# Making the weights' low halves on VectorE alone in a two-layer hybrid decoder on one core

## The chip, the cores and the metric

The kernel runs on one core of one Trainium2 chip. What is measured is the device time of one execution in microseconds. Five engines are spoken of: TensorE (PE, with PEld for its weight loads), VectorE (DVE), ScalarE (ACT), GpSimd (POOL) and SyncE (SP), which issues most of the DMAs.

## What is computed

The reference runs two layers of a decoder on 256 positions of width 1024, in float32. Cut to its spine:

```python
def reference(x, mem, ...):
    for layer in range(2):
        h = rmsnorm(x, norm_mix[layer])
        if layer == 0:   # RG-LRU and sparse attention side by side
            mix = even_mixer(h, ...)
        else:            # Mamba-2: conv of x/B/C, chunked scan, gate, grouped norm
            mix = mamba2(h, od_w_in[0], od_conv_w[0], ...)
        x = x + mix
        x = x + cross_attn(rmsnorm(x, norm_cross[layer]), rmsnorm(mem, norm_mem[layer]), ...)
        h = rmsnorm(x, norm_ffn[layer])
        x = x + (swiglu(h, ff_w13[0], ff_w2[0]) if layer == 0   # FF 2816
                 else moe(h, moe_router[0], moe_w13[0], moe_w2[0]))  # top 2 of 8, FF 3584
    return x
```

## The kernel before

**Weights.** All large weights are cut on the host into units of 128 x 2048 float32 (1 MB). The class `Stream` brings them in the order in which they are used: `_dma` issues the loads on SP into buffers named `raw`; `pieces` (line 214) turns a unit into a high half `wh` and a low half `wl`; `limit` sets how many units may stand split ahead of their use (up to three). `advance` splits as many as there is room for, `one` a single unit, and `get` hands a unit to its product and calls `advance`. A high half is the weight rounded to the matmul's format by ScalarE (line 223), and a low half is what the rounding lost, `raw - wh`, one subtraction with both inputs and the output in SBUF (line 226). "A low" below is one such subtraction for one half unit, 128 x 1024 elements. Every product is then three matmuls (`mm3`, lines 433 to 435): high by high, and the two cross terms of high and low. So TensorE needs both halves of a unit before it gets past the unit's first matmuls. Units with a gain (the cross-attention's key and value weights) take their low from line 235, on VectorE, and the units `gates`, `ck` and `cv` aren't split at all.

**Who makes a low half** is said by a table of cuts, three numbers for each piece: first column, last column, and 0 for VectorE or 1 for GpSimd. Line 238 chooses the table:

- `CUTS_D`, the default: first half VectorE, second half GpSimd.
- `CUTS_P`: both halves GpSimd. For `POOL_UNITS`, the first four units `xs` of the Mamba mixer's x part, and for the `one` in the second layer's cross-attention (line 1417).
- `CUTS_M` and `CUTS_E`: both halves VectorE. For unit 3 of the first mixer's output, for the units split inside `pair` (line 580), and for all units of the experts (`m13`, `m2`).
- `CUTS_0`, four quarters on GpSimd, for the very first unit (line 1180); and two units at the experts' entry have both halves on GpSimd by tables of their own (in `ahead` of the router and in the experts' opening).

**Order.** Nothing reorders the program: each engine's instructions run in the order in which the Python emits them. A step of the kernel (a product, an attention stage) calls `get`, whose `advance` emits the lows of the unit three ahead at that point, so a low stands in its engine's queue between instructions of the stage that happens to run then.

**The stages that the change touches**, in their order: the first mixer, the first cross-attention, the dense SwiGLU, the Mamba mixer and the second cross-attention. After that the experts run for more than half of the span, with all their lows on VectorE already.

**The Mamba mixer.** First come the products for the step sizes dt and for B and C (`bc`), then per group of channels x (`xs`) and the gate z. A convolution follows each `bc` and `xs` product (`conv`, lines 844 to 850): ScalarE scales the accumulator in PSUM, then VectorE adds three shifted copies of it (line 848: one input in PSUM, one in SBUF), and `run_between` puts one step of the softplus of dt (line 812, all in SBUF) after each. One step later `conv_silu` (line 1608) has ScalarE's tanh and VectorE's product of it with the convolution (line 1609, all in SBUF). The accumulators in PSUM are four, so TensorE can run ahead of this chain by that much. The softplus ends in `m_a`, which TensorE needs for the cumulative sums (line 1575). While a `bc` unit is multiplied, an `xs` unit is split.

Of each group then `mb_xt` (line 1657 on) makes `m_xd` and `m_xs` (lines 1667, 1670, on VectorE) and `m_y` (line 1669, on GpSimd) from the transposed x, TensorE takes `m_xd` at line 1697 and `m_xs` at line 1709.

**Cross-attention.** `soft` takes row maxima from PSUM on VectorE (`x_mx`, line 1375), `post` divides, `av_t` transposes; the query product `xq` is put between these steps, and the next units are split meanwhile. A norm's `xn` (line 474) and the split of its transposed result (`hl`, line 430) come before the products that follow.

Of the kernel before, what the change touches and what calls it, by code (L numbers as in the profile page):

```python
# [29 lines left out]
NRAW, NRAW1, NRAW2, NRAW3 = 4, 2, 5, 2  # L30
TRACE = None
CUTS_0 = ((0, 512, 1), (512, 1024, 1), (1024, 1536, 1), (1536, 2048, 1))
CUTS_D = ((0, 1024, 0), (1024, 2048, 1))
CUTS_P = ((0, 1024, 1), (1024, 2048, 1))
POOL_UNITS = [("xs", u) for u in range(4)]
CUTS_M = ((0, 1024, 0), (1024, 2048, 0))
CUTS_E = ((0, 1024, 0), (1024, 2048, 0))

PCOLS = dict(mix0=8, mix1=8, cross0=8, cross1=8, mem0=8, mem1=8, ffn0=8, ffn1=8,
             rgw=32, rgb=8, ba=8, bx=8, lam=8, qn=1, kn=3, xqn=2, xkn=2, pos=32,  # L40
# [138 lines left out]
class Stream:  # L179
# [34 lines left out]
    def pieces(self, cuts=None):  # L214
        i = self.ns
        r = self.raw.pop(i)
        h = self.hip.tile([128, 2048], F32R, name="wh")
        l = self.lop.tile([128, 2048], F32R, name="wl")
        self.split[i] = (h, l)
        nc, gains = self.nc, self.gains(self.order[i])  # L220

        def high(a, b):
            nc.scalar.activation(h[:, a:b], r[:, a:b], AF.Copy)  # L223

        def low(a, b, eng):
            (nc.gpsimd if eng else nc.vector).tensor_tensor(l[:, a:b], r[:, a:b], h[:, a:b].bitcast(F32),  # L226
                                                            op=OP.subtract)

        def high_gain(k, g):
            s = slice(k * 512, (k + 1) * 512)  # L230
            nc.scalar.activation(h[:, s], r[:, s], AF.Copy, scale=g)

        def low_gain(k, g):
            s = slice(k * 512, (k + 1) * 512)
            nc.vector.scalar_tensor_tensor(l[:, s], r[:, s], g, h[:, s].bitcast(F32), op0=OP.mult, op1=OP.subtract)
        if gains:
            return [(partial(high_gain, k, g), partial(low_gain, k, g)) for k, g in enumerate(gains)]
        cuts = cuts or (CUTS_M if self.order[i] == ("wo0", 3) else CUTS_E if self.order[i][0] in ("m13", "m2") else CUTS_P if self.order[i] in POOL_UNITS else CUTS_D)
        return [(partial(high, a, b), partial(low, a, b, eng)) for a, b, eng in cuts]

    def limit(self, n):
# [48 lines left out]
def _program(ctx, nc, tc, d, upto):  # L290
# [74 lines left out]
    def add(fn, *units, heavy=False):  # L365
        steps.append((units, fn, heavy or bool(units)))
# [16 lines left out]
    ST = {}  # L383
# [17 lines left out]
    def U(*key, keep=False, lazy=False):  # L401
        return ST["S"].get(tuple(key), keep, lazy)

    def release():
        ST["S"].held -= 1
# [4 lines left out]
    def taken(f):  # L410
        n = len(steps)
        f()
        new = steps[n:]
        del steps[n:]
        return new
# [16 lines left out]
    def mm3(ps, wh, wl, xh, xl, first, last):  # L432
        mm(ps, wh, xh, start=first, stop=False)  # L433
        mm(ps, wh, xl, start=False, stop=False)  # L434
        mm(ps, wl, xh, start=False, stop=last)  # L435
# [7 lines left out]
    def acc():  # L443
        return accp.tile([128, 512], F32, name="acc")
# [4 lines left out]
    H = {}  # L449
# [101 lines left out]
    def pair(ka, kb, emit_a, emit_b, evac, mid=None, wide=True, ahead=None, lazy=False):  # L551
        st = {}
        both = (0, 1) if wide else (0,)

        def s1():
            st["a"] = U(*ka, keep=True, lazy=lazy)
            emit_a(st["a"], 0, both)

        def s2():
            st["b"] = U(*kb, keep=True, lazy=lazy)  # L560
            emit_b(st["b"], 0, both)
            for c in both:
                evac(0, c)

        def s3():
            emit_a(st["a"], 1, both)
            release()
            if mid is None or ahead:
                (ahead or ST["S"].advance)()
            if wide:  # L570
                emit_b(st["b"], 1, (0,))
                evac(1, 0)

        def s4():
            S, cut = ST["S"], []
            if mid is not None:
                mid()
                S._dma()
                if S.room():
                    cut = S.pieces(CUTS_M)  # L580
                    for h, _ in cut:
                        h()
                    n = len(cut) // 2
                    hooks.extend([[l for _, l in cut[:n]], [l for _, l in cut[n:]]])
            emit_b(st["b"], 1, both[-1:])
            evac(1, both[-1])
            release()
            if cut:
                assert not hooks
                S.finish()  # L590
        add(s1, ka)
        add(s2, kb)
        add(s3, heavy=True)
        add(s4, heavy=True)

    def ws(key, h, evac, pool=None):
# [53 lines left out]
    def pair512(name, c, h, evac, ahead=None):  # L650
        st = {}

        def emit(kh):
            def f(w, t, cs):
                xh, xl = h()
                wh, wl = w
                if kh == 0:
                    st[t] = acc()
                for k in range(4):
                    kk = kh * 4 + k  # L660
                    s = slice(t * 128, (t + 1) * 128)
                    ws_ = slice(k * 512, (k + 1) * 512)
                    mm3(st[t], xh[:, kk, s], xl[:, kk, s], wh[:, ws_], wl[:, ws_], kk == 0, kk == 7)
            return f
        pair((name, 2 * c), (name, 2 * c + 1), emit(0), emit(1),
             lambda t, c: evac(t, st[t]), wide=False, lazy=True, ahead=ahead)

    def as1024(name, u0, n, h, evac, mid=None, ahead=None):
        st = {}

        def emit(i):
            def f(w, t, cs):
                xh, xl = h()
                wh, wl = w
                if i == 0 and t + cs[0] == 0:
                    st["ps"] = [acc() for _ in range(4)]
                for c in cs:
                    for k in range(2):
                        kk = i * 2 + k
                        s = slice(t * 128, (t + 1) * 128)  # L680
                        ws_ = slice(k * 1024 + c * 512, k * 1024 + (c + 1) * 512)
                        mm3(st["ps"][t * 2 + c], xh[:, kk, s], xl[:, kk, s], wh[:, ws_], wl[:, ws_],
                            i == 0 and k == 0, i == n - 1 and k == 1)
            return f

        def whole(i):
            def f():
                w = U(name, u0 + i)
                emit(i)(w, 0, (0, 1))
                emit(i)(w, 1, (0, 1))  # L690
            add(f, (name, u0 + i))
        for i in range(n - 2):
            whole(i)
        pair((name, u0 + n - 2), (name, u0 + n - 1), emit(n - 2), emit(n - 1),
             lambda t, c: evac(t, c, st["ps"][2 * t + c]), mid, ahead=ahead)
# [631 lines left out]
    def cross(l, after, mid, fill1, fill2, fill3, late, early=(), ahead=None):  # L1327
        X_ = ExitStack()
        c = {}
        key = f"c{l}"  # L1330
# [73 lines left out]
        def av_m(t):  # L1404
# [9 lines left out]
                s = slice(t * 128, (t + 1) * 128)  # L1414
                split_to(c["h"][:, :, s], c["l"][:, :, s], po)
            return f
        xq = taken(lambda: pair512(f"xq{l}", 0, lambda: H[key], ev_xq, lambda: ST["S"].one(CUTS_P if l else None)))
        wo = taken(lambda: as1024(f"xo{l}", 0, 2, lambda: (c["h"], c["l"]), after, mid, ahead))
        add(open_)
        gap(xq[:2])  # L1420
# [4 lines left out]
        def open2():  # L1425
# [23 lines left out]
        add(lambda: X_.close())  # L1449

    cross(0, lambda t, c, ps: add_X(t, c, ps, N["f0"], (0,)), lambda: N["f0"].tr(0), m1[:1], m1[1:2], m1[2:3],
          lambda c: N["f0"].scale(0))
    if upto == "cross0":
# [411 lines left out]
    def rt_late(c):  # L1865
# [15 lines left out]
        ve.tensor_copy(idb, identb)  # L1881

    cross(1, rt_after, None, [], [], [], rt_late, (rt_open,), ahead)
    if upto == "cross1":
        add(lambda: RT.close())
# [400 lines left out]
```

## Time and profile before

| | |
|---|---|
| median of three runs | 1771.21 us (1771.08 to 1772.83) |
| the profiled execution | 1771.26 us |
| its span | 1769.5 us |
| TensorE's mean granted clock, share of full | 0.988 |
| busy TensorE / its weight loads | 1709.3 / 1436.1 us |
| busy VectorE / ScalarE / GpSimd | 1384.9 / 1162.3 / 346.7 us |
| moved over the span | 489.60 MB, 276 GB/s of HBM traffic |

The busy time of an engine is the time in which one of its instructions ran, stalls inside an instruction included. A wait is time in which an engine had its next instruction but not what that instruction needs. The granted clock of a stretch is the share of TensorE's full rate that the chip allowed in it. In rows with "xN" N instructions of one kind stand together.

### The profile page before, as it was taken

The page shows a single profiled execution, that of the slowest core. Times are in us where ns is not written, and L with a number is a line of the kernel's source. Part 1 is how long each engine was busy: PE and PEld are TensorE (multiplying, and loading weights), DVE is VectorE, ACT ScalarE, POOL GpSimd, SP SyncE. Part 2 cuts the span into 40 slices and gives each one's busy share as a digit, 9 for nine tenths or more (in the row PEclk, how much of TensorE's full clock was granted, in tenths as well). Part 3 has the DMA queues.
Part 4 walks back from the last instruction along what each step waited for, and adds up shares of the span by engine and source line. Part 5 has one row for each costly group of instructions (what it writes and reads, how often), then busy time and mean ns, then how long its engine had stood idle before and what let it go on. Part 6 is the DMA issues. An engine that isn't in the chain of part 4 may idle for free.

```text
span 1769.5 us, 23965 instructions
## 1 busy us (share of the span) xinstructions
PE 1709.3 (97%) x9048; PEld 1436.1 (81%) x9048; DVE 1384.9 (78%) x1669; ACT 1162.3 (66%) x1637; POOL 346.7 (20%) x191
## 2 busy tenths in 40 slices
PE   7999999999998999979999999999999999999997
PEld 7797677899988788767888888888888888888885
DVE  6686756533357898668989999999999999999996
ACT  5646545544444666367777877777777777777874
POOL 4333142444434345345000000000000000000000
PEclk9999999999999999899999999999999999999999
DMA  8555244455563243558999999999999999999980
GB/s 310 215 210 189 94 143 143 162 181 193 179 228 124 93 145 141 204 202 302 386 377 389 370 379 394 368 383 392 374 379 376 374 394 372 385 385 367 402 337 26
DMA packets 74812, 489.60 MB, mean 277 GB/s; under 512 B 11200, under 2 KB 11712, under 8 KB 17472
## 3 DMA queue, kind: packets, MB, share of 16 engines
q1 hardware_dynamic: 67968, 474.36, 70.5%
q0 software_dynamic: 3024, 11.01, 1.7%
q10 hardware_dynamic: 3696, 2.62, 0.5%
q8 instruction: 73, 1.20, 0.3%
q14 instruction: 51, 0.42, 0.1%
HBM read 482.19 MB, written 5.77 MB: 276 GB/s over the span
## 4 chain that ended last, share of the span: by engine, by line
PE 81%; DVE 11%; ACT 4%; issue 2%; POOL 1%; DMA 0%; SPq 0%; ACTq 0%; DVEq 0%; POOLq 0%
PE gu L433 11%; PE gu L435 11%; PE gu L434 11%; PE out L433 6%; PE out L435 6%; PE out L434 6%; PE acc L435 5%; PE acc L433 5%; PE acc L434 5%; PE aux L434 2%; PE aux L435 2%; PE aux L433 2%; DVE wl L226 2%; PE misc L2066 1%; DVE m_y L848 1%
## 5 line engine op out<-in xcount | busy, mean ns | idle before, releaser
L226 DVE TENSOR_TENSOR wl<-raw,wh 128x1024 fp32r<-128x1024 f32 x619 | 747.7, 1248 | 139.3 <-ACT wh L223 138.7
L223 ACT ACTIVATE wh<-raw 128x1024 fp32r<-128x1024 f32 (+1 forms) x722 | 723.1, 1053 | 151.6 <-PE out L435 54.5
L226 POOL TENSOR_TENSOR wl<-raw,wh 128x1024 fp32r<-128x1024 f32 (+1 forms) x103 | 258.9, 2518 | 310.7 <-ACT wh L223 292.3
L433 PE MATMUL gu<-wh,mo_x0h 128*128 128x512 f32 x448 | 178.9, 399 | 0.0
L433 PE MATMUL gu<-wh,mo_x1h 128*128 128x512 f32 x448 | 178.1, 397 | 0.0
L433 PE MATMUL out<-wh,m_xsT 128*128 128x512 f32 x448 | 175.2, 391 | 0.7 <-ACT m_xsT L429 0.7
L435 PE MATMUL gu<-wh,mo_x0l 128*128 128x512 f32 x448 | 175.2, 391 | 0.0
L434 PE MATMUL gu<-wl,mo_x0h 128*128 128x512 f32 x448 | 175.2, 391 | 0.0
L435 PE MATMUL gu<-wh,mo_x1l 128*128 128x512 f32 x448 | 174.7, 390 | 0.0
L434 PE MATMUL gu<-wl,mo_x1h 128*128 128x512 f32 x448 | 174.7, 390 | 0.0
L435 PE MATMUL out<-wh,m_xsT 128*128 128x512 f32 x448 | 174.5, 390 | 0.0
L434 PE MATMUL out<-wl,m_xsT 128*128 128x512 f32 x448 | 174.3, 389 | 0.0
L2114 POOL DMA_DIRECT2D do<-hh x7 | 4.0, 568 | 661.5 <-ACT hh L2113 661.5
L433 PE MATMUL acc<-hh,wh 128*128 128x256 f32 x416 | 122.0, 293 | 0.7 <-DVE m_M L812 0.7
L434 PE MATMUL acc<-hl,wh 128*128 128x256 f32 x416 | 119.1, 286 | 0.5 <-DVE hl L430 0.5
L435 PE MATMUL acc<-hh,wl 128*128 128x256 f32 x416 | 118.8, 286 | 0.0
L434 PE MATMUL aux<-hl,wh 128*128 128x256 f32 x352 | 99.9, 284 | 1.3 <-DVE hl L430 1.3
L433 PE MATMUL aux<-hh,wh 128*128 128x256 f32 x352 | 99.9, 284 | 0.3 <-ACT hh L429 0.3
L435 PE MATMUL aux<-hh,wl 128*128 128x256 f32 x352 | 99.7, 283 | 0.0
L435 PEld LDWEIGHTS gu<-wh,mo_x0l 128*128 128x128 f32 x448 | 84.5, 189 | 18.4
L435 PEld LDWEIGHTS gu<-wh,mo_x1l 128*128 128x128 f32 x448 | 84.1, 188 | 18.3
L433 PEld LDWEIGHTS out<-wh,m_xsT 128*128 128x128 f32 x448 | 84.1, 188 | 18.1 <-ACT m_xsT L429 0.9
(455 smaller groups left out, 3390.5 us busy)
## 6 DMA issues: line engine op xcount, KB each, us to landing
raw<-m SPq DMA_DIRECT2D x265, 1024.0 KB, 7.3
raw<-wd SPq DMA_DIRECT2D x110, 1024.0 KB, 4.8
m_yy<-m SPq DMA_DIRECT2D x24, 1024.0 KB, 7.1
kv<-m SPq DMA_DIRECT2D x24, 1024.0 KB, 7.2
hl<-m SPq DMA_DIRECT2D x23, 1024.0 KB, 7.8
do<-hh POOLq DMA_DIRECT2D x7, 512.0 KB, 8.4
X<-x SPq DMA_DIRECT2D x4, 256.0 KB, 4.8
raw<-wd SPq DMA_DIRECT2D x2, 512.0 KB, 7.7
```

What stands on the lines that cost most here:

```text
L223: nc.scalar.activation(h[:, a:b], r[:, a:b], AF.Copy)
L226: (nc.gpsimd if eng else nc.vector).tensor_tensor(l[:, a:b], r[:, a:b], h[:, a:b].bitcast(F32), op=OP.subtract)
L433: mm(ps, wh, xh, start=first, stop=False)
L434: mm(ps, wh, xl, start=False, stop=False)
L435: mm(ps, wl, xh, start=False, stop=last)
L848: ve.scalar_tensor_tensor(dst[:, s:], src[:, :256 - s], wname(j), dst[:, s:], op0=OP.mult, op1=OP.add)
L2066: pe.transpose(ps[:, j * 128:(j + 1) * 128], mo["hd", e, c][:, j * 128:(j + 1) * 128], ident)
L2114: gp.dma_start(mo["do"][e * 128:(e + 1) * 128], o)
```

## The change

One table, `CUTS`, with both halves on VectorE, takes the place of `CUTS_D`, `CUTS_P`, `CUTS_M`, `CUTS_E` and `POOL_UNITS`. `CUTS_0` for the first unit stays, and so do the two units at the experts' entry. The changed file is four lines shorter, so its line 222 is line 226 of before, and so on down.

```diff
--- before.py
+++ after.py
@@ -30,11 +30,7 @@
 NRAW, NRAW1, NRAW2, NRAW3 = 4, 2, 5, 2
 TRACE = None
 CUTS_0 = ((0, 512, 1), (512, 1024, 1), (1024, 1536, 1), (1536, 2048, 1))
-CUTS_D = ((0, 1024, 0), (1024, 2048, 1))
-CUTS_P = ((0, 1024, 1), (1024, 2048, 1))
-POOL_UNITS = [("xs", u) for u in range(4)]
-CUTS_M = ((0, 1024, 0), (1024, 2048, 0))
-CUTS_E = ((0, 1024, 0), (1024, 2048, 0))
+CUTS = ((0, 1024, 0), (1024, 2048, 0))
 
 PCOLS = dict(mix0=8, mix1=8, cross0=8, cross1=8, mem0=8, mem1=8, ffn0=8, ffn1=8,
              rgw=32, rgb=8, ba=8, bx=8, lam=8, qn=1, kn=3, xqn=2, xkn=2, pos=32,
@@ -235,7 +231,7 @@
             nc.vector.scalar_tensor_tensor(l[:, s], r[:, s], g, h[:, s].bitcast(F32), op0=OP.mult, op1=OP.subtract)
         if gains:
             return [(partial(high_gain, k, g), partial(low_gain, k, g)) for k, g in enumerate(gains)]
-        cuts = cuts or (CUTS_M if self.order[i] == ("wo0", 3) else CUTS_E if self.order[i][0] in ("m13", "m2") else CUTS_P if self.order[i] in POOL_UNITS else CUTS_D)
+        cuts = cuts or CUTS
         return [(partial(high, a, b), partial(low, a, b, eng)) for a, b, eng in cuts]
 
     def limit(self, n):
@@ -577,7 +573,7 @@
                 mid()
                 S._dma()
                 if S.room():
-                    cut = S.pieces(CUTS_M)
+                    cut = S.pieces()
                     for h, _ in cut:
                         h()
                     n = len(cut) // 2
@@ -1414,7 +1410,7 @@
                 s = slice(t * 128, (t + 1) * 128)
                 split_to(c["h"][:, :, s], c["l"][:, :, s], po)
             return f
-        xq = taken(lambda: pair512(f"xq{l}", 0, lambda: H[key], ev_xq, lambda: ST["S"].one(CUTS_P if l else None)))
+        xq = taken(lambda: pair512(f"xq{l}", 0, lambda: H[key], ev_xq, lambda: ST["S"].one()))
         wo = taken(lambda: as1024(f"xo{l}", 0, 2, lambda: (c["h"], c["l"]), after, mid, ahead))
         add(open_)
         gap(xq[:2])
```

On GpSimd the lows of 128 x 1024 go from 99 to 4; VectorE gets 95 more. TensorE, ScalarE and SP issue the same instructions in the same order as before. Three places on VectorE:

The first place is the product of the last `bc` units (`m_BC` is B and C after their activation, `m_y` the convolution, `m_M` the scratch of the softplus). Before:

```order
L848 SCALAR_TENSOR_TENSOR m_y_5283<-acc,m_hw,m_y_5283 128x253
L812 SCALAR_TENSOR_TENSOR m_M<-m_M 128x64
L1609 SCALAR_TENSOR_TENSOR m_BC<-m_th,m_y_5247 128x256
L848 SCALAR_TENSOR_TENSOR m_y_5327<-acc,m_hw,m_y_5327 128x255
L812 SCALAR_TENSOR_TENSOR m_M<-m_M 128x64
L848 SCALAR_TENSOR_TENSOR m_y_5327<-acc,m_hw,m_y_5327 128x254
L812 SCALAR_TENSOR_TENSOR m_M<-m_M 128x64
L848 SCALAR_TENSOR_TENSOR m_y_5327<-acc,m_hw,m_y_5327 128x253
L812 TENSOR_SCALAR m_M<-m_M 128x64
L1609 SCALAR_TENSOR_TENSOR m_BC<-m_th,m_y_5283 128x256
```

And now:

```order
L844 SCALAR_TENSOR_TENSOR m_y_5283<-acc,m_hw,m_y_5283 128x253
L808 SCALAR_TENSOR_TENSOR m_M<-m_M 128x64
L1605 SCALAR_TENSOR_TENSOR m_BC<-m_th,m_y_5247 128x256
L222 TENSOR_TENSOR wl<-raw,wh 128x1024 x2
L844 SCALAR_TENSOR_TENSOR m_y_5327<-acc,m_hw,m_y_5327 128x255
L808 SCALAR_TENSOR_TENSOR m_M<-m_M 128x64
L844 SCALAR_TENSOR_TENSOR m_y_5327<-acc,m_hw,m_y_5327 128x254
L808 SCALAR_TENSOR_TENSOR m_M<-m_M 128x64
L844 SCALAR_TENSOR_TENSOR m_y_5327<-acc,m_hw,m_y_5327 128x253
L808 TENSOR_SCALAR m_M<-m_M 128x64
L1605 SCALAR_TENSOR_TENSOR m_BC<-m_th,m_y_5283 128x256
L844 SCALAR_TENSOR_TENSOR m_y_5363<-acc,m_hw,m_y_5363 128x255
```

Two lows of an `xs` unit, GpSimd's before, stand between line 1609 (now 1605) and the next convolution's first addition. It is so after every second block of `bc`.

The second place is the last group's `mb_xt`, with `m_sz` the gate and `m_yy` the normed output. Before:

```order
L1645 TENSOR_TENSOR m_M<-m_M,m_G 128x512 x4
L226 TENSOR_TENSOR wl<-raw,wh 128x1024
L1609 SCALAR_TENSOR_TENSOR m_xsT<-m_th,m_y_6572 128x256
L1743 SCALAR_TENSOR_TENSOR m_yy<-aux,par,m_yy 128x256 x4
L226 TENSOR_TENSOR wl<-raw,wh 128x1024
L1685 SCALAR_TENSOR_TENSOR m_sz<-m_sz,acc 128x512 x2
L1667 TENSOR_TENSOR m_xd<-m_xs,m_dd 128x512
L1670 TENSOR_TENSOR m_xs<-m_xs,md_dt 128x512 x2
L226 TENSOR_TENSOR wl<-raw,wh 128x1024
```

And now:

```order
L1641 TENSOR_TENSOR m_M<-m_M,m_G 128x512 x4
L222 TENSOR_TENSOR wl<-raw,wh 128x1024 x2
L1605 SCALAR_TENSOR_TENSOR m_xsT<-m_th,m_y_6572 128x256
L1739 SCALAR_TENSOR_TENSOR m_yy<-aux,par,m_yy 128x256 x4
L222 TENSOR_TENSOR wl<-raw,wh 128x1024 x2
L1681 SCALAR_TENSOR_TENSOR m_sz<-m_sz,acc 128x512 x2
L1663 TENSOR_TENSOR m_xd<-m_xs,m_dd 128x512
L1666 TENSOR_TENSOR m_xs<-m_xs,md_dt 128x512 x2
L222 TENSOR_TENSOR wl<-raw,wh 128x1024 x2
```

Each single low has become two, one after the other; the second ones were GpSimd's. `m_y` of `mb_xt` (now line 1665) stays on GpSimd.

The third place is the second cross-attention's first `soft`. Before:

```order
L425 TENSOR_SCALAR rs_tmp<-x_ss 128x4
L1375 TENSOR_REDUCE x_mx<-aux 128x2 x2
L1377 SCALAR_TENSOR_TENSOR x_mx<-x_mx,x_rq 128x4
L1344 COPY x_l<-acc 128x512
L1360 COPY m_xsT<-aux 128x4x128
L425 TENSOR_SCALAR rs_tmp<-x_ss 128x4
L1386 RECIPROCAL x_den<-x_den 128x4
```

And now:

```order
L421 TENSOR_SCALAR rs_tmp<-x_ss 128x4
L222 TENSOR_TENSOR wl<-raw,wh 128x1024 x2
L1371 TENSOR_REDUCE x_mx<-aux 128x2 x2
L1373 SCALAR_TENSOR_TENSOR x_mx<-x_mx,x_rq 128x4
L1340 COPY x_l<-acc 128x512
L1356 COPY m_xsT<-aux 128x4x128
L421 TENSOR_SCALAR rs_tmp<-x_ss 128x4
L1382 RECIPROCAL x_den<-x_den 128x4
```

Two lows, GpSimd's before, now stand ahead of the row maxima `x_mx`.

## Rows read from the trace of the kernel before

**Rows 1.** Page of the profile, part 1: busy us, share of the span, instructions.
```profile
PE 1709.3 (97%) x9048; PEld 1436.1 (81%) x9048; DVE 1384.9 (78%) x1669; ACT 1162.3 (66%) x1637; POOL 346.7 (20%) x191
```

**Rows 2.** Waits of TensorE (waiter, releaser: us in total, times, longest).
```profile
PE aux L1575 <- DVE m_a L812: 3.5, 1, 3.5
PE acc L434 <- POOL wl L226: 2.5, 1, 2.5
PE aux L1593 <- DVE m_M L1586: 2.4, 1, 2.4
PE aux L435 <- DVE m_th L430: 2.2, 1, 2.2
PE aux L1697 <- DVE m_xd L1667: 2.1, 1, 2.1
...
PE aux L434 <- DVE hl L430: 1.3, 1, 1.3
...
PE aux L1709 <- DVE m_xs L1670: 1.1, 1, 1.1
...
PE aux L948 <- DVE c_hs L937: 0.7, 1, 0.7
```

**Rows 3.** Stretches: us; busy of PE, PEld, DVE, ACT, POOL; clock, DMA share, GB/s.
```profile
546.00:552.00 6.00, 6.00 (x52) 6.00 (x51) 5.81 (x11) 3.35 (x6) 2.44 (x1) 1.00 0.21 61
550.00:600.00 50.00, 41.58 (x306) 38.90 (x305) 44.39 (x75) 25.58 (x54) 24.47 (x11) 0.93 0.31 107
600.00:650.00 50.00, 48.76 (x303) 41.91 (x302) 46.21 (x63) 28.84 (x57) 21.62 (x10) 1.00 0.45 160
350.00:400.00 50.00, 50.00 (x358) 47.02 (x357) 16.11 (x21) 22.23 (x30) 20.98 (x10) 1.00 0.53 189
```

**Rows 4.** Timeline of GpSimd in the bc products (start us, us).
```profile
552.24 4.78 POOL L226 TENSOR_TENSOR wl<-raw,wh 128x1024 fp32r<-128x1024 f32 x2 [2.74 <-ACT wh L223]
```

**Rows 5.** Timeline of VectorE there, same columns.
```profile
552.52 2.22 DVE L812 SCALAR_TENSOR_TENSOR m_M<-m_M 128x64 f32<-128x64 f32 x1
554.66 2.64 DVE L1609 SCALAR_TENSOR_TENSOR m_BC<-m_th,m_y 128x256 f32<-128x256 f32 x1
557.22 0.47 DVE L848 SCALAR_TENSOR_TENSOR m_y<-acc,m_hw,m_y 128x255 f32<-128x255 f32 x1
...
558.66 0.21 DVE L812 SCALAR_TENSOR_TENSOR m_M<-m_M 128x64 f32<-128x64 f32 x1
...
565.25 0.47 DVE L848 SCALAR_TENSOR_TENSOR m_y<-acc,m_hw,m_y 128x255 f32<-128x255 f32 x1
```

**Rows 6.** Lines 1609, 848, 226 and 1670 on VectorE: ns min/median/max.
```profile
L1609 DVE SCALAR_TENSOR_TENSOR m_BC<-m_th,m_y x8: 409/812/2640, 545.1 to 572.3; 128x256 f32<-128x256 f32 x8
L848 DVE SCALAR_TENSOR_TENSOR m_y<-acc,m_hw,m_y x72: 377/481/484, 538.2 to 689.7; 128x255 f32<-128x255 f32 x24, 128x254 f32<-128x254 f32 x24, 128x253 f32<-128x253 f32 x24
L226 DVE TENSOR_TENSOR wl<-raw,wh x619: 1199/1218/3414, 19.7 to 1753.1; 128x1024 fp32r<-128x1024 f32 x155
L1670 DVE TENSOR_TENSOR m_xs<-m_xs,md_dt x8: 677/1996/2870, 593.3 to 714.3; 128x512 f32<-128x512 f32 x8
```

**Rows 7.** Timeline of VectorE, last group of the Mamba mixer.
```profile
706.29 2.89 DVE L226 TENSOR_TENSOR wl<-raw,wh 128x1024 fp32r<-128x1024 f32 x1
...
710.30 1.33 DVE L1667 TENSOR_TENSOR m_xd<-m_xs,m_dd 128x512 f32<-128x512 f32 x1
711.73 3.24 DVE L1670 TENSOR_TENSOR m_xs<-m_xs,md_dt 128x512 f32<-128x512 f32 x2
```

**Rows 8.** Timeline of VectorE, end of the first cross-attention.
```profile
317.02 3.56 DVE L474 SCALAR_TENSOR_TENSOR xn<-X,n_rs,f_h 128x512 f32<-128x512 f32 x2
320.50 4.55 DVE L226 TENSOR_TENSOR wl<-raw,wh 128x1024 fp32r<-128x1024 f32 x2
```

**Rows 9.** Stretches of half clock, columns as in rows 3.
```profile
326.50:329.90 3.40, 3.40 (x18) 3.40 (x17) 0.88 (x1) 1.13 (x1) 3.11 (x1) 0.50 1.00 424
...
712.20:725.80 13.60, 12.50 (x43) 9.69 (x42) 7.62 (x9) 0.85 (x2) 1.63 (x1) 0.50 0.22 77
```

## The prediction

> **What bounds the kernel now.** I read the page's busy times first, then TensorE's waits, then windows, and the timelines only where a wait pointed. TensorE is busy 97% of the span [rows 1], so a change on other engines can give back only what TensorE waits, and what it loses at a lower clock. The list of waits [rows 2] names VectorE or GpSimd for nearly every wait in the stages that the change touches; the eight that I use add up to 15.8 us. None is for a transfer of weights, so what the change does to the DMAs' start I cost at nothing: buffers come free when a unit is split, TensorE is what is short, and the DMA share in the four stretches shown is 0.21 to 0.53 [rows 3].
>
> The second thing to see is why VectorE is late. Where GpSimd makes two lows of 2.4 us each, from 552.24 to 557.02 [rows 4], VectorE's step of the softplus takes 2.22 us, and line 1609 takes 2.64 [rows 5]. Undisturbed, the same step takes 0.21 [rows 5] and line 1609 0.41 [rows 6]. These work on SBUF alone. Line 848, which takes one input from PSUM, never took more than 0.484 in 72 instructions [rows 6], whatever GpSimd did. So a low on GpSimd isn't free work beside VectorE: each of these two held VectorE up by (2.22 − 0.21 + 2.64 − 0.41) / 2 = 2.1 us. On VectorE a low takes 1.218 (median of 619 [rows 6]).
>
> **The change, part by part.** It removes 95 lows from GpSimd and adds 95 × 1.218 = 115.7 us of work to VectorE, less the stalls that go. ScalarE's highs stay, in the same order. The sum is made against the profiled execution of 1771.26 us (span 1769.5 and 1.8 around it), which lies 0.05 above the median of the runs.
>
> *Dense SwiGLU.* VectorE is busy 16.1 of 50 us there and TensorE all of them [rows 3]. The cover is VectorE's 34 idle us; GpSimd's ten instructions there, as lows of VectorE, would cost 12.2 [rows 3]. I take 0; without that cover each low would cost its 1.2.
>
> *Products of bc and the first xs.* From one unit's first addition to the next unit's, VectorE's chain takes 565.25 − 557.22 = 8.03 us [rows 5]. TensorE's own pace is 6.00 / 52, some 0.12 us a matmul [rows 3], so 48 × 0.12 = 5.76 for a unit. Without the stalls and with two lows of its own VectorE's cycle is 8.03 − 4.2 + 2.44 = 6.27. Two cycles have this form before `m_a` is wanted, so the wait at line 1575 should fall by 2 × (8.03 − 6.27) = 3.5, which is the whole of it. What comes late next is still the same chain, since 6.27 is over 5.76. Bounds: 0, if the lows put back what the stalls took, and the 5.9 of both waits there (lines 1575 and 1593 [rows 2]). I take **−3.5**.
>
> *The products ahead of bc* wait 2.2 for `m_th` [rows 2]. Its subtraction is of the same size and kind as line 1609; I price its stall likewise at 2.64 − 0.41 = 2.2, and a low now ahead of it at 1.2: **−1.0**, between −2.2 and +1.2.
>
> *End of the first cross-attention.* TensorE waits 1.3 for `hl` [rows 2]. Ahead of it two `xn` take 3.56 where two such operations on SBUF take 2 × 0.68 undisturbed (the least of line 1670 [rows 6]), and two lows take 4.55 for 2.44 [rows 8]. These 4.3 go, and two lows of 2.44 come in: 1.9 earlier, of which the wait can use 1.3. The high half of `hl` is ScalarE's and isn't moved, so I take **−1.0**, between −1.3 and +2.4.
>
> *Last group's* `m_xd` *and* `m_xs`. Before them one low took 2.89 and now two take 2.44; `m_xd` took 1.33 and `m_xs` twice 1.62 [rows 7], undisturbed 0.68 each [rows 6]. That makes `m_xd` 0.45 + 0.65 = 1.1 earlier and `m_xs` 1.9 more. The waits are 2.1 and 1.1 [rows 2]: **−2.2** (1.1 of the first, all of the second), between 0 and −3.2. GpSimd keeps `m_y`, which can still hold `m_xd` up; the earlier groups have other products to run and I cost them at nothing, with TensorE at 48.76 of 50 us [rows 3].
>
> *Second cross-attention.* The 2.5 of waiting for a GpSimd low [rows 2] goes. In exchange two lows stand ahead of `x_mx` and one ahead of a copy that a transpose waits for; I let half of the 2.44 and the 1.2 reach TensorE: −2.5 + 1.2 + 1.2, **0**, between −2.5 and +3.7.
>
> *First mixer.* `c_hs` gets one more low ahead of it where TensorE already waits 0.7 [rows 2]: **+1.2**, between 0 and 1.2. Elsewhere in that mixer TensorE has no listed wait for a low, and I take 0.
>
> Together −3.5 − 1.0 − 1.0 − 2.2 + 0 + 1.2 = −6.5.
>
> *The clock.* Five stretches ran at half the full rate, four of about 3.4 us and one of 13.6 (the first and the last of them: [rows 9]). TensorE was busy 3.4 and 12.5 us in these two, and at full clock would have needed half of that: 1.7 and 6.2. All five together are 4 × 1.7 + 6.2 = 13 at most. They came shortly after TensorE had waited: the first after the 1.3 for `hl`, the third after the 3.5 for `m_a`, the last after the 2.1 and 1.1 of the last group. Where I take a wait away, I expect the stretch behind it to go: bounds 0 and −13. I take the first and third whole and half of the last (its wait shrinks but stays): −1.7 − 1.7 − 3.1 = **−6.5**.
>
> The sum is 1771.26 − 6.5 − 6.5 = **1758.3 us**. Its low end is the bc waits gone whole (−2.4 more) and all five stretches gone (−6.5 more): 1749.
>
> **The rivals.**
> (a) *The waits shrink, and the half clock stays*, because TensorE still waits a little in the same places. For it: every place keeps some wait in my sums. Against: three of the stretches follow just the waits that shrink most. 1771.3 − 6.5 = 1764.8 us.
>
> (b) *No change that shows.* The lows of VectorE stand whole ahead of operations that read PSUM, which never stalled, so that such an operation is 1.2 later per low and nothing comes back for it. If that is so at four of TensorE's waits, 4 × 1.2 gives back 4.9 of the 6.5, and with the clock as it was the time is 1769.6; with one or two places more it is up to 1773. For it: line 848, `x_mx` and `c_hs` are of that kind. Against: in the bc products the stalls are in the same chain as the lows.
>
> (c) *Slower: VectorE becomes the bound from 550 to 650 us.* It is busy 44.39 + 46.21 = 90.6 of 100 us [rows 3], the most of all the stretches that I looked at. GpSimd is busy 46.1 there, at 2.39 a low [rows 4] at most 19 lows. If VectorE's own work were really 90.6, 19 × 1.218 = 23.1 more would make 113.7 and the kernel 13.7 slower, 1785. It decides at 13.7 / 19 = 0.72 us: if a low that leaves GpSimd frees less than that of VectorE's time, VectorE is the bound; at half of it, the time is 1771.3 + 6.9 = 1778. For it: GpSimd works only 20% of the span [rows 1] and takes work that VectorE hardly has room for. Against: 2.1 us freed per low in the two cycles that I measured, and the median 2.0 against a least of 0.68 on line 1670 [rows 6].
>
> One rule speaks for (c). The Trainium skill, Perfetto Trace Analysis, section "Optimizing Scalar/DVE Operations", says that where VectorE is saturated it may pay to offload work to ScalarE or even to GpSimd; by that rule the lows should stay where they are, and the time would be that of (c). The trace disagrees as far as rows 5 go, and the same section's next sentence allows for it: the two engines share a read port, so moving work between them might not help.
>
> That the change doesn't do what it says isn't a rival: the instructions show 95 lows moved.
>
> **How the numbers follow.** The forecast has 0.50, (a) 0.20, (b) 0.15, (c) 0.15. A measurement of this kernel can tell 0.2%, 3.5 us, from no change, so faster means under 1767.7: the forecast and (a), 0.70. (b) is the same, 0.15, and (c) slower, 0.15. The range goes from 1749 to 1772: it holds the forecast with the bounds of its clock term, (a) and most of (b), and leaves out (c).
>
> **What would show it.** In the changed profile no low runs on GpSimd between the first unit and the experts' entry; line 1609 (now 1605) has a median near 0.41 and a largest well under 2; a cycle of bc takes 6.3 us; the wait for `m_a` is under 1 us; the wait for a GpSimd low is gone; and of the half-clock stretches at least two of the five are missing. VectorE's busy time should rise by clearly less than 115.7 us. If line 1609 still takes 2.6 with nothing on GpSimd, my reading of the stalls is wrong. If VectorE is 95% busy or more from 550 to 650 us and TensorE less than before, (c) is right. If the waits are shorter and the span fell by less than 8, the clock term was wrong.

## The result, and the profile after

The changed kernel takes **1751.48 us** (median of four, 1751.32 to 1751.91) against 1771.84 for the kernel before beside it (1771.08 to 1772.83). The ratio is **0.9893, 95% interval 0.9881 to 0.9905**: 20.4 us, or 1.1%, faster. In a later comparison the ratio was 0.9895 (0.9880 to 0.9910). The prediction of 1758.3 had the direction and the mechanism; the gain is half as large again as its 13 us.

Busy times of the page after (columns as in [rows 1]):

```profile
PE 1700.9 (97%) x9048; PEld 1427.0 (82%) x9048; DVE 1419.8 (81%) x1764; ACT 1161.9 (66%) x1637; POOL 106.6 (6%) x96
```

GpSimd went from 346.7 us to 106.6, and VectorE from 1384.9 [rows 1] to 1419.8. That is 34.9 us more for 95 × 1.22 = 116 us of added work, so by this difference some 81 us of VectorE's busy time before were stalls: 81 / 95 = 0.85 us for each low moved, taken over the whole kernel. The operations that stalled, in the view of single lines (ns min/median/max):

```profile
L1605 DVE SCALAR_TENSOR_TENSOR m_BC<-m_th,m_y x8: 416/421/425, 542.9 to 565.9; 128x256 f32<-128x256 f32 x8
```
```profile
L1666 DVE TENSOR_TENSOR m_xs<-m_xs,md_dt x8: 677/689/1347, 585.2 to 701.9; 128x512 f32<-128x512 f32 x8
```
```profile
L887 DVE SCALAR_TENSOR_TENSOR rg_nt<-rg_nt,kv x8: 399/408/421, 100.1 to 121.9; 128x256 f32<-128x256 f32 x8
```

Line 1605 (1609 before) never takes more than 0.425 us, where it reached 2.64 [rows 6]. Line 1666 has a median of 0.69 where it had 2.0 [rows 6]; it reaches 1.35 beside `m_y`, the one large operation that GpSimd kept in that stage. Line 887 belongs to the first mixer's recurrence; before, as line 891, its largest was six times as long:

```profile
L891 DVE SCALAR_TENSOR_TENSOR rg_nt<-rg_nt,kv x8: 398/419/2534, 102.0 to 125.8; 128x256 f32<-128x256 f32 x8
```

The same stretch of the bc products on VectorE (timeline: start us, us):

```profile
550.14 2.35 DVE L222 TENSOR_TENSOR wl<-raw,wh 128x1024 fp32r<-128x1024 f32 x2
552.41 0.48 DVE L844 SCALAR_TENSOR_TENSOR m_y<-acc,m_hw,m_y 128x255 f32<-128x255 f32 x1
...
553.99 0.42 DVE L1605 SCALAR_TENSOR_TENSOR m_BC<-m_th,m_y 128x256 f32<-128x256 f32 x1
...
556.23 2.36 DVE L222 TENSOR_TENSOR wl<-raw,wh 128x1024 fp32r<-128x1024 f32 x2
558.50 0.48 DVE L844 SCALAR_TENSOR_TENSOR m_y<-acc,m_hw,m_y 128x255 f32<-128x255 f32 x1
```

From one unit's first addition to the next it is 558.50 − 552.41 = 6.09 us, for 8.03 before [rows 5] and 6.27 in the prediction, with two lows inside. TensorE's waits (us in total, times, longest):

```profile
PE aux L1589 <- DVE m_M L1582: 3.4, 1, 3.4
...
PE aux L477 <- DVE a_PT L1130: 1.9, 1, 1.9
...
PE misc L2062 <- DVE mo_sg L2055: 1.7, 1, 1.7
...
PE aux L431 <- DVE m_th L426: 0.9, 1, 0.9
...
PE aux L1693 <- DVE m_xd L1663: 0.6, 1, 0.6
...
PE aux L430 <- DVE hl L426: 0.3, 1, 0.3
```

Of the eight waits in [rows 2], those for `m_a` (3.5), for GpSimd's low (2.5), for `m_xs` (1.1) and for `c_hs` (0.7) are gone, `m_th` fell from 2.2 to 0.9, `m_xd` from 2.1 to 0.6, `hl` from 1.3 to 0.3; the one at line 1593 (now 1589) rose from 2.4 to 3.4. Longer, too, is the wait for `a_PT` at the end of the first mixer: 1.9 us where the same operation showed 0.9 before. Busy times by stretch, with the three stretches of half clock that are left in which TensorE works (columns as in [rows 3]; the granted clock is 0.50 inside such a stretch, the lower of the two levels that the rows show, and a window that reaches past it has a little more):

```profile
550.00:600.00 50.00, 45.12 (x341) 41.31 (x341) 45.34 (x90) 27.75 (x60) 2.51 (x2) 0.97 0.37 130
600.00:650.00 50.00, 49.99 (x291) 42.54 (x291) 42.12 (x65) 30.84 (x71) 3.69 (x4) 1.00 0.36 127
547.80:641.20 93.40, 88.51 (x607) 79.40 (x606) 83.27 (x152) 54.34 (x111) 5.50 (x5) 0.98 0.41 146
182.40:189.20 6.80, 6.80 (x14) 3.05 (x15) 2.94 (x5) 1.19 (x2) 0.00 (x0) 0.53 0.00 0
568.20:571.60 3.40, 2.75 (x13) 2.79 (x14) 2.73 (x6) 3.20 (x7) 0.00 (x0) 0.55 0.14 53
776.40:783.20 6.80, 4.92 (x49) 4.86 (x50) 5.23 (x17) 4.29 (x8) 2.13 (x1) 0.53 0.68 258
```

VectorE is busy 45.34 + 42.12 = 87.5 of 100 us from 550 to 650 with all the added work in it, for 90.6 before [rows 3], and TensorE does more: 45.12 and 49.99, for 41.58 and 48.76. The row from 547.80 to 641.20 holds the same 607 matmuls as 550 to 650 before. For these VectorE is busy 83.27 us, with the 16 lows that GpSimd made there before (16 × 1.22 = 19.5 us): 90.6 + 19.5 − 83.3 = 26.8 us of stalls are gone, 1.7 for each low.

TensorE runs the same 9048 matmuls in the same order in both kernels. So the start of the same matmul in the two traces, compared, tells where the time came from (in one profile of each). By place (times are those of the trace before; the third column is the prediction's waits and clock together):

| stretch, us | gained, us | predicted, us |
|---|---|---|
| first mixer, 73 to 140 | +1.4 | −1.2 |
| first mixer's end, 174 to 187 | −4.2 | 0 |
| end of the first cross-attention, 319 to 332 | +2.5 | +2.7 |
| ahead of the bc products, 508 to 536 | +2.3 | +1.0 |
| bc and first xs products, 557 to 592 | +5.8 | +5.2 |
| second group, 600 to 610 | +0.7 | 0 |
| last Mamba group, 702 to 734 | +8.9 | +5.3 |
| second cross-attention, 734 to 788 | 0.0 | 0 |
| experts' entry, 808 to 839 | +1.8 | 0 |

### The profile page after: what moved, and what is told of

It reads as the page before. It is cut to its first block, busy times and chain, and to the rows that moved or that the text cites. A ratio compares the mean times of both kernels' runs of the same rounds, so it can differ in the third digit from the quotient of the medians.

```text
span 1749.5 us, 23766 instructions
## 1 busy us (share of the span) xinstructions
PE 1700.9 (97%) x9048; PEld 1427.0 (82%) x9048; DVE 1419.8 (81%) x1764; ACT 1161.9 (66%) x1637; POOL 106.6 (6%) x96
## 4 chain that ended last, share of the span: by engine, by line
PE 84%; DVE 9%; ACT 4%; issue 1%; DMA 1%; POOL 0%; SPq 0%; ACTq 0%; DVEq 0%
PE gu L429 11%; PE gu L431 11%; PE gu L430 11%; PE acc L431 6%; PE acc L429 6%; PE acc L430 6%; PE out L429 6%; PE out L431 6%; PE out L430 6%; DVE wl L222 3%; PE aux L431 3%; PE aux L430 3%; PE aux L429 2%; PE misc L2062 1%; DVE m_y L844 1%
## 5 line engine op out<-in xcount | busy, mean ns | idle before, releaser
L222 DVE TENSOR_TENSOR wl<-raw,wh 128x1024 fp32r<-128x1024 f32 x714 | 842.8, 1227 | 124.7 <-ACT wh L219 123.9
L429 PEld LDWEIGHTS out<-wh,m_xsT 128*128 128x128 f32 x448 | 84.1, 188 | 18.2 <-ACT m_xsT L425 0.9
L431 PEld LDWEIGHTS out<-wh,m_xsT 128*128 128x128 f32 x448 | 84.1, 188 | 18.0 <-DVE m_xsT L426 0.4
L430 PEld LDWEIGHTS out<-wl,m_xsT 128*128 128x128 f32 x448 | 84.1, 188 | 17.4 <-DVE wl L222 0.3
```

## The experiments

The theory that the prediction states, **held up**: a low on GpSimd stops those operations of VectorE that work on SBUF alone for as long as it runs, some 2 us, and VectorE would make the low itself in 1.2. The rivals were a **latency** theory (TensorE gains because each low is ready sooner), and that the half clock or the later stages come as they like. Ratios below are to the kernel before on the same chip.

**The eight lows of the bc products alone.** In the kernel before:

```diff
-POOL_UNITS = [("xs", u) for u in range(4)]
+POOL_UNITS = []
...
-        cuts = cuts or (CUTS_M if self.order[i] == ("wo0", 3) else CUTS_E if self.order[i][0] in ("m13", "m2") else CUTS_P if self.order[i] in POOL_UNITS else CUTS_D)
+        cuts = cuts or (CUTS_M if self.order[i] == ("wo0", 3) or self.order[i] in [("xs", u) for u in range(4)] else CUTS_E if self.order[i][0] in ("m13", "m2") else CUTS_P if self.order[i] in POOL_UNITS else CUTS_D)
```

> The kernel before, with only the eight lows of the units xs 0 to 3 moved to VectorE (they are the ones made while bc is multiplied). Held-up theory: line 1609 goes back to 0.42 us in the bc products, the cycle of a bc unit falls from 8.03 to about 6.3, the wait for m_a goes, and the time falls by 3.5 us of waiting plus 1.7 to 3.4 us of half clock, so 5 to 7 us, to about 1765. Rival, a latency theory (TensorE gains because a low is ready in 1.2 instead of 2.4 us): nothing waits for these lows, so the time stays within 1 us of before.

1766.02 us, ratio 0.9970 (0.9959 to 0.9982): 5.3 us by the ratio. In the profile:

```profile
L1609 DVE SCALAR_TENSOR_TENSOR m_xsT<-m_th,m_y x16: 414/421/2528, 571.9 to 697.4; 128x256 f32<-128x256 f32 x16
L1609 DVE SCALAR_TENSOR_TENSOR m_BC<-m_th,m_y x8: 411/418/424, 545.3 to 569.0; 128x256 f32<-128x256 f32 x8
```

Line 1609 doesn't stall any more for `m_BC`, whose stage has no low on GpSimd now, and still does for `m_xsT`, whose later units have. The wait for `m_a` fell from 3.5 to 0.6 us, and from one unit's first addition to the next it is 6.1 us.

**All but these eight.** In the changed kernel:

```diff
-cuts = cuts or CUTS
+cuts = cuts or (((0, 1024, 1), (1024, 2048, 1)) if self.order[i] in [("xs", u) for u in range(4)] else CUTS)
```

> The changed kernel with those eight lows left on GpSimd. If the parts add up, the time is the changed kernel's 1751.5 plus the same 5 to 7 us, about 1757.5. If the stretches of half clock depend on each other, or the bc gain is eaten by a later wait, it is under 1754.

1757.80 us (six runs from 1755.14 to 1761.11), ratio 0.9931 (0.9919 to 0.9943): 6.7 us of the gain lost. The part alone gave 5.3 and its absence costs 6.7, so the bc products stand for 5 to 7 of the 20 us, and within that the parts add up.

**The echo.** VectorE makes every low as in the changed kernel, and GpSimd repeats eight of them for nobody:

```diff
+            if self.order[i] in [("xs", u) for u in range(4)]:
+                nc.gpsimd.tensor_tensor(self.spare, r[:, a:b], h[:, a:b].bitcast(F32), op=OP.subtract)
...
+        ST["S"].spare = p.tile([128, 1024], BF, name="m_spare")
```

> The changed kernel, in which VectorE makes all lows as there, and GpSimd beside it makes the eight subtractions of xs 0 to 3 a second time, into a spare bf16 tile that nobody reads (the outputs stay the reference's). Held-up theory: the stalls come back on top of VectorE's own lows, a bc cycle takes 6.3 + 4.2 = about 10.5 us, line 1605 again takes up to 2.6 us while line 844 stays under 0.5, and the time rises by 8 to 16 us, to 1760 to 1767. Latency theory: every low that is used is ready as early as in the changed kernel, so the time stays at 1751.5 within 1 us.

1768.96 us, ratio 0.9990 (0.9981 to 0.9999): 17 us slower than the changed kernel, by work whose result nothing reads. On GpSimd and then on VectorE:

```profile
559.91 5.07 POOL L225 TENSOR_TENSOR m_spare<-raw,wh 128x1024 bf16<-128x1024 f32 x2 [5.25 <-issue]
```
```profile
556.81 0.47 DVE L846 SCALAR_TENSOR_TENSOR m_y<-acc,m_hw,m_y 128x255 f32<-128x255 f32 x1
...
560.16 2.23 DVE L810 SCALAR_TENSOR_TENSOR m_M<-m_M 128x64 f32<-128x64 f32 x1
562.31 0.41 DVE L1608 SCALAR_TENSOR_TENSOR m_BC<-m_th,m_y 128x256 f32<-128x256 f32 x1
562.65 4.56 DVE L222 TENSOR_TENSOR wl<-raw,wh 128x1024 fp32r<-128x1024 f32 x2
567.13 0.47 DVE L846 SCALAR_TENSOR_TENSOR m_y<-acc,m_hw,m_y 128x255 f32<-128x255 f32 x1
```
```profile
L846 DVE SCALAR_TENSOR_TENSOR m_y<-acc,m_hw,m_y x72: 382/480/485, 536.4 to 697.6; 128x255 f32<-128x255 f32 x24, 128x254 f32<-128x254 f32 x24, 128x253 f32<-128x253 f32 x24
```

While GpSimd runs from 559.91 to 564.98, the softplus' step takes 2.23 us, and the pair of lows behind it 4.56 for 2.35. Line 846, the convolution from PSUM, still has its largest under 0.49. The cycle is 567.13 − 556.81 = 10.32 us, for the 10.5 expected. This decides between held up and latency at this place. VectorE makes every low of this stage, as in the changed kernel, and the time is lost all the same. A pair of lows does end later now, because it is held up itself, but TensorE waits for none of them here; the longest such wait in the list of TensorE's waits is one in the experts:

```profile
PE out L432 <- DVE wl L222: 0.5, 1, 0.5
```

Elsewhere latency isn't nothing: in the second cross-attention TensorE waited 2.5 us for a low of GpSimd before [rows 2]. The rise is 1 us above the 8 to 16 expected: four units paid, not the two or three that I had counted, and there are four stretches of half clock from 559 to 600 us.

**The dense SwiGLU.** In the changed kernel its second halves back on GpSimd:

```diff
+cuts = cuts or (((0, 1024, 0), (1024, 2048, 1)) if self.order[i][0] in ("f13", "f2") else CUTS)
```

> The changed kernel with the second half of every dense SwiGLU unit (f13 and f2, 33 units) back on GpSimd. By the prediction these lows are worth nothing on either engine: 1751.5 within 1 us, with the same stretches of half clock. If a low's latency or a stall in that stage counts, it is 2 us or more slower.

1754.18 us, ratio 0.9907 (0.9892 to 0.9921): 2.5 us above the changed kernel by the ratios, with overlapping intervals. By its size alone this meets the "2 us or more" that was to speak against the forecast, so it takes the starts of the matmuls to see where it comes from. By them nothing is lost from 332 to 790 us; 2.6 are lost at the experts' entry, where the code is the same (more on that below), and 0.7 of them come back by 830. At 322 to 332, at the edge of the stage, 1.0 is lost, and there a wait is back at its size of before:

```profile
PE aux L430 <- DVE hl L426: 1.3, 1, 1.3
```

No half clock follows it here, where the kernel before has 3.4 us of it [rows 9]. So inside a stage with room on VectorE the lows are worth nothing, as forecast, and at its edge about 1 us.

**The Mamba mixer's other units.** In the changed kernel:

```diff
+cuts = cuts or (((0, 1024, 0), (1024, 2048, 1)) if self.order[i][0] in ("z", "xs", "bc", "wo1") and self.order[i] not in [("xs", u) for u in range(4)] else CUTS)
```

> The changed kernel with the second halves of the Mamba mixer's units (z, bc, xs from the fifth on, and its output's wo1) back on GpSimd; xs 0 to 3 stay on VectorE. Held-up theory: in the last group m_xd and m_xs wait for GpSimd's lows again (2 to 3 us), the long stretch of half clock near 712 comes back (up to 6.8 us), and the time rises by 7 to 11 us, to about 1760. Rival, that the group gained only because the kernel ahead of it moved: the time stays under 1755.

1765.01 us, ratio 0.9962 (0.9948 to 0.9975): 12 us lost, the largest part of all, and more than expected. TensorE's waits:

```profile
PE aux L1693 <- DVE m_xd L1663: 2.2, 1, 2.2
PE aux L431 <- DVE m_th L426: 2.2, 1, 2.2
...
PE aux L1705 <- DVE m_xs L1666: 1.7, 1, 1.7
...
PE acc L430 <- POOL wl L222: 1.4, 1, 1.4
```

`m_xd`, `m_th` and `m_xs` wait as before, and so does a matmul for a low of GpSimd. The long stretch of half clock is back:

```profile
709.00:719.20 10.20, 9.18 (x36) 8.08 (x37) 4.26 (x6) 0.00 (x1) 0.33 (x1) 0.53 0.29 103
```

From the starts, 8.2 us are lost in the last group, 2.4 ahead of the bc products, which I hadn't counted for these units, 1.8 at the experts' entry, and 1.3 in two small pieces.

**The two units at the experts' entry.** In the changed kernel, both on VectorE too:

```diff
-for h, l in ST["S"].pieces(((0, 1024, 1), (1024, 2048, 1))):
+for h, l in ST["S"].pieces():
...
-cut = S.pieces(((0, 1024, 1), (1024, 2048, 1)))
+cut = S.pieces()
```

> The changed kernel with the two units at the experts' entry on VectorE too, so that GpSimd makes no low after the first unit. Held-up theory: GpSimd's two lows there hold up a norm factor on GpSimd's own queue by 1.1 us, but on VectorE they stand ahead of two additions to the residual that the router waits for (2.4 us), so 0 to 2 us slower than the changed kernel. Rival, that any low on GpSimd costs: 1 to 2 us faster.

1756.98 us, ratio 0.9926 (0.9913 to 0.9940), beside 0.9895 for the changed kernel on the same chip: 5.5 us slower, where I expected 0 to 2. The wait that I expected is there:

```profile
PE aux L1825 <- DVE X L695: 1.5, 1, 1.5
```

It comes from the addition to the residual, now behind two lows on VectorE, and the half clock behind it lasts 13.7 us, where two profiles of the changed kernel have 6.8 and 10.2. So "any low on GpSimd costs" is wrong: here, where TensorE waits for VectorE's next work and that reads PSUM, the low is better on GpSimd.

**The loss at the first mixer's end.** The changed kernel beside the next two, and two ways to take the wait for `a_PT` away: the first mixer's second halves back on GpSimd, and the first copy of each attention tile on ScalarE.

```diff
+cuts = cuts or (((0, 1024, 0), (1024, 2048, 1)) if self.order[i][0] in ("rgx", "rgg", "q", "c", "kv", "wo0") and self.order[i] != ("wo0", 3) else CUTS)
```

```diff
-            if i % 2 == 0:
+            if i % 2 == 0 and i:
                 ve.tensor_copy(st["T", i][:w], tp[:w])
```

> The changed kernel itself, for comparison on the same chip: 1751.5 within 1.5 us, and a stretch of half clock near 182 us, where the kernel before has none.

> The changed kernel with the second halves of the first mixer's units back on GpSimd, as before. Theory that TensorE comes 1 us too early to the copies of a_PT, waits 1.9 instead of 0.9 us there and then loses 3.4 us to half clock: the stretch near 182 goes, the 1.4 us gained earlier in the mixer go too, so 1.5 to 3 us faster than the changed kernel, about 1749. Rival, that the stretch comes by chance: same as the changed kernel or 1 to 2 us slower.

> The changed kernel, in which the copy of the first transposed block of a_PT of every attention tile is made by ScalarE instead of VectorE, where it stands behind four additions to the residual. By the theory of the wait TensorE waits under 1 us at the end of the mixer, the half clock near 182 goes, and the time falls by 3 to 5 us, to about 1747.5. Rival: ScalarE's own copy and splits queue behind it, the wait only moves, and the time is within 1 us of the changed kernel.

The changed kernel took 1752.57 us here, ratio 0.9895 (0.9880 to 0.9910), the halves 1750.44, ratio 0.9887 (0.9872 to 0.9902), the copies on ScalarE 1750.08, ratio 0.9876 (0.9860 to 0.9891). The intervals overlap; 1.4 and 3.4 us by the ratios are about what a measurement can tell. In the starts, the halves give up 1.2 us of the mixer's earlier gain and win 4.3 at its end, since TensorE then doesn't wait there for `a_PT` longer than it did before and no half clock follows at 184; but a stretch of it comes at 205 and costs 1.7. With the copies on ScalarE the wait is 1.5 instead of 1.9, the half clock 3.4 instead of 6.8 us, and 2.9 are won from there to 218 us. But the half clock at this place isn't set by the wait alone. In the experiment on line 1589 below, whose edit changes nothing before 500 us, the wait is 1.9 as in the changed kernel, and yet the half clock is 3.4 us, with 1.6 us won at this place:

```profile
PE aux L477 <- DVE a_PT L1130: 1.9, 1, 1.9
```
```profile
184.40:187.70 3.30, 3.30 (x5) 1.17 (x4) 1.09 (x2) 0.05 (x1) 0.00 (x0) 0.52 0.00 0
187.80:191.20 3.40, 3.40 (x22) 2.57 (x20) 1.84 (x3) 0.60 (x1) 0.00 (x0) 0.98 0.00 0
```

Over all profiles a wait of 0.9 has no half clock near 184 (three profiles), one of 1.5 has 3.4, none and 3.4 us, and one of 1.9 has 6.8 us in six and 3.4 in two. So a longer wait goes with more half clock there; but its length varies by 3.4 us between profiles of the same code, for a reason that no run shows, and that alone is worth 1.6 of the 2.9 us. That either edit is worth having isn't shown.

**The longest wait left, line 1589.** Its copies of `m_a` stand behind six convolution steps and two lows; here they come right behind `m_a`:

```diff
-        between.append(partial(ve.scalar_tensor_tensor, av, dt, -1.0, ea.unsqueeze(1).to_broadcast([128, 2, 32]),
-                               op0=OP.mult, op1=OP.mult))
+        def decay():
+            ve.scalar_tensor_tensor(av, dt, -1.0, ea.unsqueeze(1).to_broadcast([128, 2, 32]), op0=OP.mult, op1=OP.mult)
+            for c in range(2):
+                ve.tensor_copy(avp[:, c].rearrange("p j (b c m) -> p j b c m", b=3, c=4)[:, :, :, c],
+                               av[:, c].rearrange("p (m j) -> p j m", j=4).unsqueeze(2).to_broadcast([128, 4, 3, 8]))
+        between.append(decay)
...
-            for c in range(2):
-                ve.tensor_copy(avp[:, c].rearrange("p j (b c m) -> p j b c m", b=3, c=4)[:, :, :, c],
-                               av[:, c].rearrange("p (m j) -> p j m", j=4).unsqueeze(2).to_broadcast([128, 4, 3, 8]))
```

> The changed kernel, in which the two copies of m_a that TensorE's row sums at line 1589 wait for (3.4 us, the longest wait left in the Mamba mixer) are made right behind m_a instead of behind six convolution steps and two lows on VectorE. If that queue is the wait, it goes, and the stretch of half clock behind it with it: 3 to 5 us faster than the changed kernel. Rival: the chain behind it (the rows' high and low parts, then the G products) only waits later by as much, and the time is within 1 us of the changed kernel.

1752.59 us, ratio 0.9897 (0.9882 to 0.9913): nothing. TensorE gains 5.2 us over the changed kernel by the row sums and gives 6.2 back within the next 10:

```profile
PE aux L1635 <- DVE m_M L1593: 2.7, 1, 2.7
...
PE aux L1635 <- ACT m_G L1621: 1.8, 1, 1.8
```

The 3.4 at line 1589 became 2.7 and 1.8 at line 1635. VectorE's chain through this stage ends when it did, and TensorE waits for it in another place.

> The early copies of m_a and ScalarE's copy of a_PT together. If the two waits are independent, the sum of both gains: 5 to 7 us faster than the changed kernel, about 1745.5. If a wait that is taken away early only moves the half clock to a later place, 2 to 3 us faster.

> As the one with both, and m_y of each Mamba group (eight products of 128 x 512, 1.2 us each on GpSimd with VectorE held up beside) on VectorE too. Held-up theory: m_xd falls from 1.34 to 0.68 us, m_y adds 0.68 each behind it ahead of m_xs, so nothing within 1 us of the one with both.

With ScalarE's copies added to the early ones: 1749.71 us, ratio 0.9884 (0.9869 to 0.9899), no more than with ScalarE's copies alone (0.9876) and no sum of two. With `m_y` on VectorE as well:

```diff
-                gp.tensor_tensor(v8(y[:, c]), v8(xs[:, c]), hb(row[:, 64:96], g), op=OP.mult)
+                ve.tensor_tensor(v8(y[:, c]), v8(xs[:, c]), hb(row[:, 64:96], g), op=OP.mult)
```

1750.31 us, ratio 0.9880 (0.9865 to 0.9895), the same as without, as expected. The lowest ratio of the study is that of the copies on ScalarE alone, and no version is clear of the changed kernel.

## Why the prediction was right, and where its sizes were off

**The mechanism** was right. The stalls on operations that work on SBUF alone go when GpSimd has no low, come back when it has one that nobody needs, and the operation from PSUM is untouched in both. The price per low was right too: 10.32 us with the echo against 6.09 without is 4.2 us per pair, the 2.1 each of the prediction. It is the price where operations on SBUF alone stand beside the low, though: from 550 to 650 us it was 1.7, and over the whole kernel 0.85, which is less than the 1.22 that VectorE needs for a low. VectorE's busy time rose, and the kernel got faster because the stalls stood ahead of what TensorE waited for.

**Step by step.** *bc and first xs:* 3.5 and 1.7 predicted, 5.8 in the starts, 5.3 and 6.7 in the two experiments. (TensorE's own pace there is 48 × 6.00 / 52 = 5.54 us a unit, and not 5.76; VectorE's cycle is above both.) *End of the first cross-attention:* 1.0 and 1.7 predicted, 2.5 measured. *Second cross-attention:* 0 and 0, and by the parts that the prediction named: 2.6 came back at the wait for GpSimd's low, and 1.1 was lost ahead of it and 1.0 behind it, for the two times 1.2 (0.5 more at the first matmuls of the stretch). *Dense SwiGLU:* 0, and nothing measured inside the stage.

*Last group:* 2.2 + 3.1 predicted, 8.9 measured. The waits fell by somewhat more than forecast (2.1 + 1.1 down to 0.6), in part by luck. I let 0.65 of it come from `m_xd` itself, but `m_xd` takes 1.34 us as before, beside `m_y` on GpSimd; what went instead is a stall of line 1609 further ahead in VectorE's queue, which I hadn't counted. The stall in the timeline of before, `m_xd` in the timeline of after, and the line (now 1605) in the view of single lines after:

```profile
702.26 2.53 DVE L1609 SCALAR_TENSOR_TENSOR m_xsT<-m_th,m_y 128x256 f32<-128x256 f32 x1
```
```profile
699.89 1.34 DVE L1663 TENSOR_TENSOR m_xd<-m_xs,m_dd 128x512 f32<-128x512 f32 x1
```
```profile
L1605 DVE SCALAR_TENSOR_TENSOR m_xsT<-m_th,m_y x16: 414/417/425, 568.8 to 694.5; 128x256 f32<-128x256 f32 x16
```

So the mis-sized term is the clock's, "half of the last (its wait shrinks but stays)": the whole stretch of 13.6 us went, which is 6.2, and the experiment that brings the waits back brings back 10 us of half clock. *Ahead of bc:* 1.0 predicted, 2.3 net measured; the wait fell by the 1.3 that I had about priced, and the half clock that stood at 531 went too, which I had left standing.

*First mixer:* the step that failed is the one that said that `c_hs` "gets one more low ahead of it", for +1.2. Before, VectorE had been held up in line 891 ahead of it, up to 2.53 us at a time. Those stalls had no wait of TensorE beside them, so I counted nothing; but they are what made VectorE late at `c_hs`, which starts at 130.7 now and started at 134.2. The loss became a gain: 0.9 at `c_hs`, and with 0.4 more at 77 us, where TensorE waited 0.7 for `a_sq` before and 0.3 now, the 1.4 of the table. It didn't stay: TensorE came earlier to the end of the mixer, waited 1.9 us instead of 0.9 for `a_PT`, and ran 6.8 us at half clock, where it had run none. That is the 4.2 lost, and no step of mine looked for a place that gets worse because TensorE comes to it sooner.

*Half clock:* I counted five stretches and there were seven (an eighth, at the very end of both spans, has no work of TensorE in it). These two of the kernel before lie at the experts' entry, beyond the stages at which I looked (columns as in rows 3):

```profile
794.00:800.80 6.80, 4.79 (x48) 4.74 (x49) 5.35 (x17) 4.27 (x8) 1.96 (x1) 0.51 0.68 255
818.00:821.40 3.40, 3.40 (x12) 2.72 (x10) 3.40 (x3) 2.49 (x3) 3.32 (x3) 0.50 0.91 318
```

The half of TensorE's busy time in all seven is 13 + (4.79 + 3.40) / 2 = 17 us; in the three of after it is (6.80 + 2.75 + 4.92) / 2 = 7. So I estimate that about 10 of the 20 us came back through the clock, and about 10 through waits; I had 6.5 and 6.5. It is an estimate from one profile of each kernel: a second profile of the changed kernel has 10.2 us of half clock at the experts' entry, for the 6.8 of this one.

**The rivals.** (a), shorter waits and the same half clock, is out: five of the seven stretches are gone and one is new. (b) would need the lows to stand whole ahead of PSUM operations at four of TensorE's waits; that does happen at the experts' entry when its lows are moved (up to 5.5 us) and at the two places of the second cross-attention (1.1 and 1.0 us lost), so the point of the rival was real, but not at enough places of this change. (c), VectorE as the bound, is out by its own condition: a moved low had to free 0.72 us, and it freed 1.7 for the same matmuls, so VectorE's busy time there fell. The Trainium skill's advice (Perfetto Trace Analysis, "Optimizing Scalar/DVE Operations") to offload a saturated VectorE even to GpSimd would have kept the slower kernel here; its next sentence, that the two engines share a read port and moving work between them might not help, is the one that the echo bears out, with 17 us lost.

**What stays open.** The experts' entry differs by 2.5 us between profiles: where TensorE's wait at line 2062 is 2.5 to 2.7 us, a stretch of half clock follows at about 800 to 820, and where it is 1.7 or less, none does. Both were seen with the same code there (2.7 with the dense SwiGLU's halves, 1.7 in the changed kernel). So the 1.8 us of the table's last row can't be put down to the change, and what sets that wait wasn't tried. Neither was the length of a stretch of half clock explained, which differs between profiles of the same code (first mixer's end, 6.8 and 3.4 us), nor were the cross-attentions' units put back by themselves.

## What to carry to other kernels

Compare the duration of an operation with its own minimum before calling an engine full: a VectorE that was busy 90.6 of 100 us here was stalled for some 30% of that by a GpSimd that seemed to help it, and taking work from GpSimd then freed VectorE. Price a piece of work on GpSimd by what it holds up at its place: that was 2.1 us per low in the bc products, against 1.2 for doing it on VectorE, and nothing in the dense SwiGLU. Where VectorE's own next work is awaited and reads PSUM, as at the experts' entry, the work was better left on GpSimd. When TensorE is short of time, count the half clock after a wait with the wait, and look for the places to which TensorE will now come too early.

## What the runs showed that I had not expected

Subtractions on GpSimd whose result nothing reads cost nearly as much as the whole change gains: eight of them, 17 of the 20 us. Half clock was, by the estimate above, as large a part of the gain as waiting, and where a wait grew by 1 us (for `a_PT`, 0.9 to 1.9), 3.4 or 6.8 us of it followed. And the longest wait of a stage, 3.4 us, could be taken away for nothing at all, because the chain behind it ended when it did.
